# Convolution module of a streaming encoder: shifted copies made inside SBUF, one bank for the layer norm's sums, a new order of steps

## The chip, the cores and the metric

The kernel runs on one core of a Trainium2 chip. The time is the device time of one execution in microseconds (us), launch to end; a run's number is that of one execution, and the median of several runs is compared. TensorE is called PE, VectorE DVE, ScalarE ACT, GpSimd POOL and SyncE SP in the rows. SP computes nothing here: its queue starts every DMA.

## The reference

One step of an encoder with four layers, on 512 new tokens of one stream and 64 of another (576 columns in all), width 1024, float32. Each layer is a token mixer and a feed-forward block. The mixer of layer 1 is the convolution module that the change touches:

```
a, g = split(h @ w_pw1 + b_pw1)           # 1024 -> 2 x 1024
glu  = a * sigmoid(g)
xp   = concat([state, glu])               # 30 earlier rows in front
c    = silu(layernorm(dwconv31(xp)))      # 31 taps for each channel, layer norm over channels
y    = c @ w_pw2 + b_pw2                  # state out: the last 30 rows of xp
```

Layers 0 and 3 attend in a window, layer 2 is a gated MLP; every layer is followed by a feed-forward block with a convolution of width 3.

## The kernel before, in words

Channels lie on the 128 partitions, tokens along the free axis; a matrix of width 1024 is eight tiles c = 0 to 7 of 128 channels. The tokens are worked on in two halves of 256 and 320 columns. Matrix products are made in three passes of a split float32 format (lines 287 to 289): weights arrive by DMA in a stage buffer (two of them), ACT casts the high part (L256), DVE subtracts it for the low part (L259), and PE multiplies high by high, high by low and low by high, for eight slices of the contraction: 24 matmuls a product.

**The convolution module** (`conv_module`, L1272). For each tile c there are four products of pw1 (two halves by two branches). DVE scales each pair by the norm ("turn", L1313), ACT takes the sigmoid (L1316) and DVE gates (L1322) into the gated tile `v_glu`, 636 columns: 30 zeros, the prompt, 30 columns of state, the sample. The 31 taps are split. The first `4 * CPACKS[c]` run on PE in packs of four taps: for channel rows 32q to 32q+31 a copy `cp[q]` (`v_g` in the rows) holds each of the 32 rows four times, shifted by 0, 1, 2 and 3 columns, on 128 partitions, so that one matmul with a weight of 128 x 32 (a stack of four diagonals, made by DVE on L1380 from `ident4` and the columns of taps in `ct`) does four taps of 32 channels; four such matmuls, q = 0 to 3, run side by side in PE's column groups (L1404). The remaining taps run on DVE, one instruction of 606 columns each (L1395), the first of them on ACT (L1393). DVE then joins both parts (L1420).

The copies go by DRAM: one DMA writes the gated tile to `v_gd` (L1373), four DMAs read it back (L1366), each with the source pattern of 4 shifts by 32 rows by w columns.

For the layer norm over channels PE sums the joined tile and its squares with a weight of ones (L1448) into two PSUM banks, one for each half, values in rows 0 to 63 and squares in rows 64 to 127. After four tiles a rough centre is taken off (L1459, L1462, L1465); PE adds it for the later tiles (L1411 to L1413). At the end ACT copies the sums, PE transposes them, DVE works out mean and deviation, and pw2 follows.

**The order of the work** in this module is written out by hand: `CORDER` is a list of steps, a letter and a tile (a third part is a repeat count), and each engine gets its instructions in that order. The letters: R the last part of the norm (R0 steps of its chain on DVE, R1 its spread on PE, R2 a copy on ACT), H and h the load and cast of pw1's weights, l their low part, x one product, t, i, g turn, sigmoid and gate, c the write to DRAM, C the four copies, y the diagonals, b the first DVE tap (on ACT), d a tap on DVE, e a pack on PE, w the centre on PE, j the join, r and v the state's rows, m, n, u the centre, z and q squares and sums, W, O, o load, cast and low part of pw2's weights, K the table of silu. DMAs are started by SP in the order of the list as well; a DMA that has to wait holds those behind it.

PSUM has six banks for products and packs and two for the rest; 20 large buffers hold gated tiles, copies, DVE's results and joined tiles.

Of the kernel before, what the change touches and what calls it, by code (L numbers as in the profile page):

```python
# [8 lines left out]
F32 = mybir.dt.float32  # L9
# [14 lines left out]
NF = 22  # L24
NEG = -1.0e30
APART = 1
CPACKS = (5, 4, 4, 4, 4, 4, 4, 3)

CORDER = (
# [9 lines left out]
)  # L39

AORDER = (
# [92 lines left out]
def encoder_step_kernel(  # L134
# [31 lines left out]
    def mm_tile(name):  # L166
        return mmp.tile([P, 512], F32, tag="mm", name=name)

    def ms_tile(name):
        return msp.tile([P, 512], F32, tag="ms", name=name)  # L170
# [4 lines left out]
    def b_tile(name, shape, dt=F32):  # L175
        return bp.tile(shape, dt, tag="b", name=name)
# [4 lines left out]
    def w_tile(name, shape, dt=F32):  # L181
        return wp.tile(shape, dt, tag="t", name=name)
# [5 lines left out]
    ident = cp.tile([P, P], F32, tag="ident", name="ident")  # L188
    make_identity(nc, ident)
    ident4 = cp.tile([P, 32], F32, tag="ident4", name="ident4")  # L190
    G.tensor_tensor(ident4, ident[:, :32], ident[:, 32:64], ALU.add)
    for q in (64, 96):
        G.tensor_tensor(ident4, ident4, ident[:, q : q + 32], ALU.add)
    ones = cp.tile([P, P], F32, tag="ones", name="ones")
    G.memset(ones, 1.0)
    thirty2 = cp.tile([P, 1], F32, tag="thirty2", name="thirty2")
# [1075 lines left out]
    def conv_module(i, j):  # L1272
# [9 lines left out]
                packs.append((dram(conv_w_dw[j], c * P + q * 32, [[4 * D, np_], [D, 4], [1, 32]]), np_))  # L1282
        ct = columns(f"{n}_ct", [rows(conv_b_pw1, 16), rows(conv_b_dw, 8), rows(conv_ln_g, 8), rows(conv_ln_b, 8), rows(conv_b_pw2, 8), (conv_w_dw[j].rearrange("w (c p) -> (w c) p", p=P), 248), *packs], at)
        wt = ct[:, 48:296].rearrange("p (w c) -> p w c", c=8)
        stt = columns(f"{n}_st", [(state_conv[j, 0].rearrange("w (c p) -> (w c) p", p=P), 240)], 240, tag="mix").rearrange("p (w c) -> p w c", c=8)
        gl, po = {}, []
        halves, place = {}, {}
# [56 lines left out]
        class Tile:  # L1344
# [15 lines left out]
            def copies(self):  # L1360


                w = NB + self.te - 4
                self.cp = [b_tile(f"{self.m}_g{q}", [P, w]) for q in range(4)]
                for q in range(4):
                    nc.sync.dma_start(  # L1366
                        self.cp[q],
                        bass.AP(self.gd.tensor, self.gd.offset + 32 * q * 636, [[1, 4], [636, 32], [1, w]]),
                    )

            def out(self):
                self.gd = dp.tile([P, 636], F32, tag=f"glu{self.c}", name=f"{self.m}_gd")
                nc.sync.dma_start(self.gd, self.g)  # L1373

            def diagonals(self):
                self.dg = []
                for q in range(2):
                    o, np_ = four[self.c] + 2 * q * self.packs, 2 * self.packs
                    t = h_tile(f"{self.m}_dg{q}", F32)[:, : np_ * 32].rearrange("p (n m) -> p n m", m=32)
                    V.tensor_tensor(t, ident4[:, None, :].to_broadcast([P, np_, 32]), ct[:, o : o + np_, None].to_broadcast([P, np_, 32]), ALU.mult)  # L1380
                    self.dg += [t[:, : self.packs], t[:, self.packs :]]

            def tap(self, kind):
# [58 lines left out]
            def squares(self):  # L1442

                if not squared:
                    sums.extend(mm_tile(f"{n}_sums{hf}") for hf in range(2))
                for z, (a, e) in enumerate(((0, 256), (256, NT))):
                    for at, t in enumerate((ds[self.c], self.sq)):
                        T.matmul(  # L1448
                            sums[z][64 * at : 64 * at + 64, : e - a], ones[:, :64], t[:, a:e],
                            start=(not squared), stop=(len(squared) == KD - 1),  # L1450
                        )
                squared.add(self.c)
# [46 lines left out]
        def do(kind, c):  # L1499
            if kind == "K":  # L1500
                S.activation(sp.tile([P, 1], F32, tag="mu", name=f"{n}_silu"), ones[:, :1], AF.Silu)
            elif kind == "R":
                if c == 0:
                    r_steps.pop(0)()
                elif c == 1:
                    steps.append(spread(f"{h.name}_1", h.r[1], 1))
                else:
                    S.copy(half(h.R, 1), steps.pop())
            elif kind in "mnu":
                if kind == "m":  # L1510
                    steps.append(centre())
                next(steps[0])
            elif kind == "H":
                q = asked[c] = asked.get(c, -1) + 1
                load(f"{n}_{c}_w{q}", conv_w_pw1[j], 0, KD, q * D + c * P, P)
            elif kind == "h":
                split(c, ws.setdefault(c, []))
            elif kind == "l":
                lows[c].pop(0)(V)
            elif kind == "W":  # L1520
                load(f"{n}_w2{c}", conv_w_pw2[j], 0, KD, c * P, P)
            elif kind == "O":
                split(("o", c), out_ws.setdefault(c, []))
            elif kind == "o":
                lows["o", c].pop(0)(V)
            elif kind == "x":
                hs = halves.setdefault(c, [])
                if not hs:
                    begin_gated(c)
                if not hs or not hs[-1].products:  # L1530
                    hs.append(Gated(c, len(hs), ws[c]))
                hs[-1].products.pop(0).all()
            elif kind in "tig":
                at = place.get((kind, c), 0)
                place[kind, c] = at + 1
                {"t": Gated.turn, "i": Gated.sigmoid, "g": Gated.gate}[kind](halves[c][at])
            else:
                t = tile_of(c)
                {
                    "b": t.vector, "c": t.out, "C": t.copies, "d": t.vector, "e": t.tensor, "y": t.diagonals, "w": t.tensor_end,  # L1540
                    "j": t.join, "r": t.state, "v": t.rows, "z": t.square, "q": t.squares,
                }[kind]()

# [18 lines left out]

        with tc.manual_schedule(engines={*ENGINES, mybir.EngineType.Activation}):
            rb, db, chains, dr = {}, {}, [], {}
            for hf in range(2):
                w, nb = HALF[hf][1], 2 + hf
                both = b_tile(f"{n}_both{hf}", [P, w])
                S.copy(both, sums[hf][:, :w])
                ps = ms_tile(f"{n}_both{hf}_t")
                for q, at in enumerate((0, P, 192)[:nb]):  # L1570
                    T.transpose(ps[:, q * P : (q + 1) * P], both[:, at : at + P], ident)
                s1, s2 = (ps[:, : nb * P].rearrange("p (b c) -> p b c", c=P)[:, :, at] for at in (0, 64))
                dm, d2, vr, dr[hf] = (sp.tile([P, 3], F32, tag=tag, name=f"{n}_{tag}{hf}")[:, :nb] for tag in ("dm", "d2", "vr", "dr"))
                r, steps_ = rsqrt_steps(f"{n}_s{hf}", vr, nb, 1.0 / D, 1e-5)
                rb[hf] = r
                chains.append([
                    lambda dm=dm, s1=s1: V.tensor_scalar(dm, s1, 1.0 / D, None, ALU.mult),
                    lambda dm=dm, s1=s1, d2=d2: V.tensor_tensor(d2, dm, s1, ALU.mult),
                    lambda vr=vr, s2=s2, d2=d2: V.tensor_tensor(vr, s2, d2, ALU.subtract),
                    *steps_,  # L1580
                    lambda dm=dm, r=r, t=dr[hf]: V.tensor_tensor(t, dm, r, ALU.mult),
                ])
# [321 lines left out]
```

## Time and profile before

| | |
|---|---|
| median of 3 runs | 2830.97 us (2828.22 to 2831.78) |
| profiled execution | 2828.47 us |
| its span, first to last instruction | 2826.7 us |
| PE busy | 2758.0 us, 98% of the span |
| DVE busy | 1857.0 us, 66% |
| ACT busy | 1137.7 us, 40% |
| DMA | 233.31 MB, 83 GB/s in the mean |

In the profile a row names the line, the engine, the operation and the tiles (result first); a bracket tells how long the engine was idle before and what ended that. A matmul in float32 shows as two instructions. [...]

### The profile page before, as it was taken

Reading aid. Unit: us, or ns where it says so; the run is one execution under the profiler, and the core shown is the slowest. Engines: PE = TensorE matmul, PEld = TensorE weight load, DVE = VectorE, ACT = ScalarE, POOL = GpSimd, SP = SyncE. Lnnn points to the kernel's source line nnn. Section 1 sums busy time; section 2 is a strip of 40 time slices with the busy share of each in tenths; the row PEclk is TensorE's granted clock in tenths of the full one; section 3 lists DMA queues with packets and bytes.
Section 4 is the critical chain, followed back from the end, with each engine's and each line's share of the span. In section 5 each row is a group of like instructions: output and inputs, shape, how many; then the busy total and the mean of one; then the engine's idle time right before and its main releaser. Section 6 shows DMA issues by size and latency. Waiting matters only on the chain.

```text
span 2826.7 us, 52768 instructions
## 1 busy us (share of the span) xinstructions
PE 2758.0 (98%) x20841; PEld 2633.4 (93%) x20841; DVE 1857.0 (66%) x4194; ACT 1137.7 (40%) x2392; POOL 384.7 (14%) x937
## 2 busy tenths in 40 slices
PE   8999999999887999999999999999999999999998
PEld 7889999998666899999999999999999878999998
DVE  5668666657776576667657667666666676766674
ACT  4755433334124453233434324432333674533343
POOL 3122111110000021111002011211110121211111
PEclk9999999999888999999999999999999999999999
DMA  5322322322431232222233221322222421322221
GB/s 168 86 52 71 93 87 75 90 66 64 124 119 47 75 90 83 83 84 86 68 91 101 75 77 55 90 83 82 85 81 79 106 50 47 95 86 82 83 83 58
DMA packets 358413, 233.31 MB, mean 83 GB/s; under 512 B 42802, under 2 KB 347670, under 8 KB 358038
## 3 DMA queue, kind: packets, MB, share of 16 engines
q1 hardware_dynamic: 358166, 229.94, 28.0%
q8 instruction: 164, 2.69, 0.4%
q14 instruction: 83, 0.68, 0.1%
HBM read 223.00 MB, written 10.05 MB: 82 GB/s over the span
## 4 chain that ended last, share of the span: by engine, by line
PE 92%; DMA 4%; DVE 2%; SPq 1%; issue 1%; ACT 0%; POOL 0%; POOLq 0%; ACTq 0%; DVEq 0%
PE f_p L287 13%; PE f_p L289 13%; PE f_p L288 13%; PE o_p L287 10%; PE o_p L288 9%; PE o_p L289 9%; DMA v_g<-v_gd 3%; PE v_pc L1404 1%; PE m_u_p L287 1%; PE m_u_p L289 1%; PE m_u_p L288 1%; PE m_vp L287 1%; PE t_sp L1117 1%; PE m_vp L288 1%; PE m_vp L289 1%; PE t_qp L287 1%
## 5 line engine op out<-in xcount | busy, mean ns | idle before, releaser
L287 PE MATMUL f_p<-n_hi,f_w_h 128*128 128x320 f32 (+1 forms) x2688 | 799.1, 297 | 0.0
L289 PE MATMUL f_p<-n_hi,f_w_l 128*128 128x320 f32 (+1 forms) x2688 | 797.3, 297 | 0.0
L288 PE MATMUL f_p<-n_lo,f_w_h 128*128 128x320 f32 (+1 forms) x2688 | 797.3, 297 | 0.0
L287 PEld LDWEIGHTS f_p<-n_hi,f_w_h 128*128 128x128 f32 x2688 | 510.0, 190 | 4.5 <-issue 4.1
L288 PEld LDWEIGHTS f_p<-n_lo,f_w_h 128*128 128x128 f32 x2688 | 510.1, 190 | 0.0
L289 PEld LDWEIGHTS f_p<-n_hi,f_w_l 128*128 128x128 f32 x2688 | 510.0, 190 | 0.0
L287 PE MATMUL o_p<-f_ah,f_d_h 128*128 128x256 f32 (+1 forms) x1408 | 419.5, 298 | 2.8 <-ACT f_d_h L256 2.8
L288 PE MATMUL o_p<-f_al,f_d_h 128*128 128x256 f32 (+1 forms) x1408 | 418.4, 297 | 0.0
L289 PE MATMUL o_p<-f_ah,f_d_l 128*128 128x256 f32 (+1 forms) x1408 | 417.4, 297 | 0.0
L256 ACT CAST f_w_h<-f_w_f 128x512 fp32r<-128x512 f32 x352 | 200.7, 618 | 495.7 <-PE f_p L288 235.8
L537 DVE TENSOR_TENSOR o_y<-o_p,o_y 128x256 f32<-128x256 f32 (+1 forms) x432 | 195.2, 455 | 262.5 <-PE o_p L289 261.2
L800 DVE TENSOR_TENSOR f_ub<-f_p,n_R 128x256 f32<-128x256 f32 x352 | 148.3, 423 | 286.6 <-PE f_p L289 282.0
L287 PEld LDWEIGHTS o_p<-f_ah,f_d_h 128*128 128x128 f32 x1408 | 268.6, 191 | 4.5 <-ACT f_d_h L256 2.9
L288 PEld LDWEIGHTS o_p<-f_al,f_d_h 128*128 128x128 f32 x1408 | 268.7, 191 | 0.2 <-issue 0.2
L289 PEld LDWEIGHTS o_p<-f_ah,f_d_l 128*128 128x128 f32 x1408 | 268.2, 191 | 0.2 <-issue 0.2
L259 DVE TENSOR_TENSOR f_w_l<-f_w_f,f_w_h 128x512 fp32r<-128x512 f32 x352 | 229.1, 688 | 19.8 <-ACT f_w_h L256 17.6
L256 ACT CAST f_d_h<-f_d_f 128x512 fp32r<-128x512 f32 x176 | 101.3, 619 | 231.8 <-PE f_p L288 171.4
L812 DVE SCALAR_TENSOR_TENSOR f_c<-f_ub,f_ct,f_c 128x578 f32<-128x578 f32 x176 | 144.0, 821 | 38.3 <-ACT f_c L811 38.3
L808 POOL COPY f_fo<-f_ub 128x2 f32<-128x2 f32 x176 | 46.1, 262 | 888.2 <-DVE f_ub L800 880.8
L811 ACT ACTIVATE f_c<-f_ub,f_ct 128x578 f32<-128x578 f32 x176 | 150.9, 863 | 1.4 <-POOL f_fo L808 0.7
L821 ACT CAST f_ah<-f_a 128x576 fp32r<-128x576 f32 x88 | 59.3, 674 | 218.6 <-DVE f_a L818 218.6
L813 DVE SCALAR_TENSOR_TENSOR f_c<-f_ub,f_ct,f_c 128x578 f32<-128x578 f32 x176 | 143.5, 817 | 2.8
(374 smaller groups left out, 5632.0 us busy)
## 6 DMA issues: line engine op xcount, KB each, us to landing
f_w_f<-in_ffn_w_up_dram SPq DMA_DIRECT2D x176, 512.0 KB
f_d_f<-in_ffn_w_down_dram SPq DMA_DIRECT2D x80, 512.0 KB
v_w_f<-in_conv_w_pw_dram SPq DMA_DIRECT2D x24, 512.0 KB
t_wq_f<-in_attn_w_qkv_dram SPq DMA_DIRECT2D x32, 256.0 KB
t_wo_f<-in_attn_w_o_dram SPq DMA_DIRECT2D x32, 256.0 KB
m_wv_f<-in_cmlp_w_in_dram SPq DMA_DIRECT2D x16, 512.0 KB
m_u_w_f<-in_cmlp_w_in_dram SPq DMA_DIRECT2D x16, 512.0 KB
m_wo_f<-in_cmlp_w_out_dram SPq DMA_DIRECT2D x16, 512.0 KB
```

The source lines that it names most:

```text
L256: S.copy(hi[:, a:e], st[:, a:e])
L259: eng.tensor_tensor(lo[:, a:e], st[:, a:e], hi[:, a:e].bitcast(F32), ALU.subtract)
L287: T.matmul(ps, lh, rh, start=(i == 0), stop=False)
L288: T.matmul(ps, lh, rl, start=False, stop=False)
L289: T.matmul(ps, ll, rh, start=False, stop=(i == n - 1))
L537: V.tensor_tensor(ys, ps, ys, ALU.add)
L800: V.tensor_tensor(ub[q][:, b : b + 256], ps[q]()[:, :256], h.R[:, hf * 256 : hf * 256 + 256], ALU.mult)
L808: G.tensor_copy(fo[:, 0, :, c], ub[q][:, 512:514])
L811: S.activation(y, ub[q][:, 2:580], AF.Identity, bias=ct[:, 3, c : c + 1], scale=ct[:, 2, c : c + 1])
L812: V.scalar_tensor_tensor(y, ub[q][:, 1:579], ct[:, 1, c : c + 1], y, ALU.mult, ALU.add)
L813: V.scalar_tensor_tensor(y, ub[q][:, 0:578], ct[:, 0, c : c + 1], y, ALU.mult, ALU.add)
L821: S.copy(a_hi[p], am)
```

## The change

The gated tile is no longer written to DRAM: four DMAs copy from SBUF to SBUF, one for each block of 32 channel rows, with a source pattern of 32 rows by 4 shifts by w columns. Row r of the block, shifted by s, now lies on partition 4r + s of the copy (before: 32s + r), so that the four shifts of a row are neighbours. `ident4` and the columns of taps are permuted to match: a permutation matrix `pm` is built from the identity, one matmul reorders the columns into `tp`, once. Tile 6 has three packs on PE instead of four, so four more of its taps run on DVE. The layer norm's sums of both halves go into four groups of 32 rows of one PSUM bank. `CORDER` is rewritten, without the step c.

```diff
-CPACKS = (5, 4, 4, 4, 4, 4, 4, 3)
+CPACKS = (5, 4, 4, 4, 4, 4, 3, 3)
 CORDER = (
-    "y0 H2 R09 y2 R1 y1 R2 H2 y4 t0 h2 t1 i0 l2 i1 g0 l2 h2 r0 c0 g1 b0 x2 l2 b1 l2 c1 d0 v0 d0 r1 d0 C0 x2 v1 d03 x2 d04 "
...
-    "z5 x7 O2 o22 e6 O3 t7 i7 o3 e6 g7 o3 b7 c7 e6 d7 e6 d72 q5 d7 C7 d72 r7 w6 d72 r6 q4 d7 v6 v7 d76 e7 d72 e7 d7 j6 e7 "
-    "z6 w7 q6 j7 z7 q7 K0"
+    "R0 H2 R08 y0 R1 y1 R2 t1 H2 t0 i1 h2 g1 y2 r1 i0 l2 b1 C1 l2 g0 h2 d1 r0 d1 b0 x2 v0 l2 v1 l2 d0 x2 d03 C0 d0 x2 d04 "
+    "x2 d0 t2 d1 i2 g2 d1 e1 H3 t2 e1 d1 i2 g2 e1 d1 b2 H3 d1 e0 d1 h3 d1 e0 d12 e0 d1 h3 e0 d12 e0 l32 e1 C2 j0 l3 x3 j1 "
+    "l3 d2 x3 d24 x3 t3 H4 d2 i3 d22 x3 d2 H4 d22 h4 d2 e2 l42 e2 d2 H5 h4 d2 e2 l42 e2 g3 H5 y5 t3 r2 h5 x4 j2 v2 l5 i3 l5 "
+    "g3 H6 h5 x4 y3 y7 b3 l52 C3 r3 t4 x4 v3 d3 i4 g4 d33 x4 h6 d34 x5 H6 t4 d3 i4 g4 x5 d3 b4 C4 d32 h6 d3 e3 t5 d3 e3 i5 "
+    "g5 y4 e3 l62 e3 l62 r4 H7 j3 x5 v4 d43 H7 d4 m0 d4 h7 d4 l72 d4 W0 x5 n1 d42 u0 x6 h7 l7 z1 l7 z3 t5 W1 q1 d4 q3 z0 i5 "
+    "d4 q0 z2 g5 x6 d4 b5 C5 d4 d5 r5 t6 q2 v5 d5 i6 x6 g6 d54 x6 O0 d54 e4 O1 t6 e4 d5 i6 g6 e5 d52 e5 d5 o0 e5 o0 o1 W2 "
+    "e5 o1 d4 w5 b6 y6 d6 e4 W3 j5 e4 d6 z5 d6 w4 d6 C6 d6 x7 j4 d6 z4 d6 x7 d63 x7 d6 t7 d6 i7 g7 d6 x7 O2 d64 e6 O3 t7 d6 "
+    "i7 e6 g7 o2 b7 e6 o2 d7 q4 C7 d7 w6 d7 r7 d7 r6 d7 q5 v6 j6 v7 d7 z6 d7 q6 d76 e7 d72 e7 d7 e7 d72 w7 o32 j7 z7 q7 K0"
 )
...
-    G.tensor_tensor(ident4, ident[:, :32], ident[:, 32:64], ALU.add)
-    for q in (64, 96):
-        G.tensor_tensor(ident4, ident4, ident[:, q : q + 32], ALU.add)
+    by_four = ident.rearrange("p (m s) -> p m s", s=4)
+    G.tensor_tensor(ident4, by_four[:, :, 0], by_four[:, :, 1], ALU.add)
+    for q in (2, 3):
+        G.tensor_tensor(ident4, ident4, by_four[:, :, q], ALU.add)
...
+        pm = w_tile(f"{n}_pm", [P, P])
+        V.tensor_copy(pm.rearrange("p (r s) -> p r s", s=4), ident.rearrange("p (s r) -> p r s", s=4))
+        pps = ms_tile(f"{n}_tp_ps")
+        T.matmul(pps[:, : at - 296], pm, ct[:, 296:at], start=True, stop=True)
+        tp = sp.tile([P, at - 296], F32, tag="tp", bufs=1, name=f"{n}_tp")
+        S.copy(tp, pps[:, : at - 296])
...
                 for q in range(4):
-                    nc.sync.dma_start(
-                        self.cp[q],
-                        bass.AP(self.gd.tensor, self.gd.offset + 32 * q * 636, [[1, 4], [636, 32], [1, w]]),
-                    )
-
-            def out(self):
-                self.gd = dp.tile([P, 636], F32, tag=f"glu{self.c}", name=f"{self.m}_gd")
-                nc.sync.dma_start(self.gd, self.g)
+                    src = self.g[32 * q : 32 * q + 32, 0:w]
+                    nc.sync.dma_start(self.cp[q], bass.AP(src.tensor, src.offset, [src.ap[0], [1, 4], [1, w]]))
...
-                    V.tensor_tensor(t, ident4[:, None, :].to_broadcast([P, np_, 32]), ct[:, o : o + np_, None].to_broadcast([P, np_, 32]), ALU.mult)
+                    V.tensor_tensor(t, ident4[:, None, :].to_broadcast([P, np_, 32]), tp[:, o : o + np_, None].to_broadcast([P, np_, 32]), ALU.mult)
...
-                    sums.extend(mm_tile(f"{n}_sums{hf}") for hf in range(2))
+                    sums.append(mm_tile(f"{n}_sums"))
                 for z, (a, e) in enumerate(((0, 256), (256, NT))):
                     for at, t in enumerate((ds[self.c], self.sq)):
+                        g = 64 * z + 32 * at
                         T.matmul(
-                            sums[z][64 * at : 64 * at + 64, : e - a], ones[:, :64], t[:, a:e],
+                            sums[0][g : g + 32, : e - a], ones[:, :32], t[:, a:e],
...
+            both = b_tile(f"{n}_both", [P, 320])
             for hf in range(2):
-                w, nb = HALF[hf][1], 2 + hf
-                both = b_tile(f"{n}_both{hf}", [P, w])
-                S.copy(both, sums[hf][:, :w])
-                ps = ms_tile(f"{n}_both{hf}_t")
-                for q, at in enumerate((0, P, 192)[:nb]):
-                    T.transpose(ps[:, q * P : (q + 1) * P], both[:, at : at + P], ident)
-                s1, s2 = (ps[:, : nb * P].rearrange("p (b c) -> p b c", c=P)[:, :, at] for at in (0, 64))
+                S.copy(both[64 * hf : 64 * hf + 64, : HALF[hf][1]], sums[0][64 * hf : 64 * hf + 64, : HALF[hf][1]])
+            ps = ms_tile(f"{n}_both_t")
+            for q in range(2):
+                T.transpose(ps[:, q * P : (q + 1) * P], both[:, q * P : (q + 1) * P], ident)
+            T.transpose(ps[:, 320:384], both[64:128, 192:320], ident[64:128, 64:128])
+            for hf in range(2):
+                nb = 2 + hf
+                s1, s2 = (ps[:, : nb * P].rearrange("p (b c) -> p b c", c=P)[:, :, at + 64 * hf] for at in (0, 32))
```

## Rows read from the trace of the kernel before

**Rows 1.** The page's first part: busy us, share of the span, instructions.

```profile
PE 2758.0 (98%) x20841; PEld 2633.4 (93%) x20841; DVE 1857.0 (66%) x4194; ACT 1137.7 (40%) x2392; POOL 384.7 (14%) x937
```

**Rows 2.** Windows: stretch, length, engines' busy us (x), PEclk, DMA share, GB/s.

```profile
699.55:884.07 184.52, 152.33 (x1208) 117.03 (x1208) 141.19 (x224) 38.88 (x70) 2.46 (x8) 0.87 0.38 117
...
693.00:884.00 191.00, 154.43 (x1220) 118.64 (x1220) 147.39 (x245) 41.94 (x75) 2.46 (x8) 0.87 0.37 113
...
1000.00:1060.00 60.00, 60.00 (x454) 60.00 (x454) 41.46 (x77) 28.68 (x54) 13.43 (x34) 1.00 0.33 97
```

**Rows 3.** Waits of PE's two rows, 690 to 890: us, times, longest.

```profile
PEld v_pc L1404 <- DMA v_g<-v_gd: 34.9, 12, 3.9
...
PE v_pc L1404 <- DMA v_g<-v_gd: 26.9, 11, 3.3
```

**Rows 4.** Waits of VectorE, 693 to 884.

```profile
DVE v_w_l L259 <- ACT v_w_h L256: 12.5, 4, 6.4
DVE v_t L1313 <- PE v_p L289: 7.3, 7, 2.5
DVE v_d L1420 <- PE v_pc L1411: 5.9, 1, 5.9
DVE v_d L1420 <- PE v_pc L1404: 5.8, 4, 3.1
...
DVE v_t L1313 <- PE v_sums L1448: 3.5, 1, 3.5
```

**Rows 5.** A window with copies alone; DMA view of 745 to 752 in 40 slices.

```profile
872.00:875.00 3.00, 1.06 (x2) 0.18 (x2) 2.75 (x6) 0.09 (x1) 0.00 (x0) 0.50 0.24 92
...
DMA  3222222222222222222222259999422222234456
GB/s 97 82 85 99 99 85 113 99 99 85 99 113 99 85 99 113 99 85 99 113 99 85 99 200 419 419 375 419 172 85 99 113 99 85 99 106 150 159 155 176
```

**Rows 6.** Timeline of SyncE's queue (start, us), the last tile.

```profile
857.17 0.35 SPq L1373 DMA_DIRECT2D v_gd<-v_glu  x1
...
860.14 2.79 SPq L1366 DMA_DIRECT2D v_g<-v_gd  x4
```

**Rows 7.** Timeline of PE: packs of tiles 1 and 7, sums of a tile.

```profile
737.59 4.29 PE L1404 MATMUL v_pc<-v_g,v_dg 128*32 128x256 f32 x64
...
859.03 0.43 PE L1448 MATMUL v_sums<-v_d,ones 128*64 128x256 f32 x1
...
859.79 0.43 PE L1448 MATMUL v_sums<-v_sq,ones 128*64 128x320 f32 x1
...
866.05 1.06 PE L1404 MATMUL v_pc<-v_g,v_dg 128*32 128x256 f32 x2 [3.12 <-DMA v_g<-v_gd]
...
875.24 4.80 PE L1404 MATMUL v_pc<-v_g,v_dg 128*32 128x256 f32 x42 [1.97 <-DMA v_g<-v_gd]
```

**Rows 8.** Timeline of VectorE: norm's chain, 18 taps, last join.

```profile
693.07 0.16 DVE L345 TENSOR_SCALAR n_v<-n_c 128x3 f32<-128x3 f32 x1 [5.40 <-PE n_c L373]
...
858.11 15.91 DVE L1395 SCALAR_TENSOR_TENSOR v_cv<-v_glu,v_ct,v_cv 128x606 f32<-128x606 f32 x18 [0.42 <-ACT v_cv L1393]
...
881.31 0.56 DVE L1420 TENSOR_TENSOR v_d<-v_pc,v_cv 128x256 f32<-128x256 f32 x2 [0.17 <-PE v_pc L1413]
```

**Rows 9.** Chain that ended last, 640 to 960 (start, us): tile 0's diagonals.

```profile
672.05 0.40 DVE v_dg L1380
...
673.31 0.40 DVE v_dg L1380
```

**Rows 10.** Timelines of ScalarE and VectorE at the stage's end.

```profile
882.66 1.28 ACT L1501 ACT_TABLE_LOAD   x1
...
884.07 0.68 ACT L1568 COPY v_both<-v_sums 128x256 f32<-128x256 f32 x2
...
884.95 0.16 DVE L1577 TENSOR_SCALAR v_dm<-v_both_t 128x2 f32<-128x2 f32 x1 [3.08 <-PE v_both_t L1571]
```

**Rows 11.** Timeline of PE behind the module's columns.

```profile
633.57 0.58 PE L287 MATMUL o_p<-f_ah,f_d_h 128*128 128x256 f32 x1 [2.77 <-ACT f_d_h L256]
```

More of the change, by code (lines that the diff above doesn't have):

```diff
@@ L1377, in diagonals @@
                 for q in range(2):
-                    o, np_ = four[self.c] + 2 * q * self.packs, 2 * self.packs
+                    o, np_ = four[self.c] - 296 + 2 * q * self.packs, 2 * self.packs
                     t = h_tile(f"{self.m}_dg{q}", F32)[:, : np_ * 32].rearrange("p (n m) -> p n m", m=32)
-                    V.tensor_tensor(t, ident4[:, None, :].to_broadcast([P, np_, 32]), ct[:, o : o + np_, None].to_broadcast([P, np_, 32]), ALU.mult)
+                    V.tensor_tensor(t, ident4[:, None, :].to_broadcast([P, np_, 32]), tp[:, o : o + np_, None].to_broadcast([P, np_, 32]), ALU.mult)
                     self.dg += [t[:, : self.packs], t[:, self.packs :]]
@@ L1539, in do @@
                 {
-                    "b": t.vector, "c": t.out, "C": t.copies, "d": t.vector, "e": t.tensor, "y": t.diagonals, "w": t.tensor_end,
+                    "b": t.vector, "C": t.copies, "d": t.vector, "e": t.tensor, "y": t.diagonals, "w": t.tensor_end,
                     "j": t.join, "r": t.state, "v": t.rows, "z": t.square, "q": t.squares,
```

6 rows, old and new, of the table CORDER are left out of this document.

## The prediction

> **What bounds the kernel now.** I read the busy shares first: PE works 98% of the span [rows 1], so in most of the kernel nothing but PE's own work could matter. The windows by stage then show where the missing 2% lies: in 699.55 to 884.07, the body of the convolution module, PE is busy 152.3 of 184.5 us at a granted clock of 0.87, while a dense stretch of the next layer gives 60.0 of 60.0 at 1.00 [rows 2]. So the change is worth what this stage can lose, and I looked for the wait that ends last there. PE's waits have one large cause: it waits 34.9 + 26.9 = 61.8 us (some of it counted on both of PE's rows) for the shifted copies v_g that come back from DRAM [rows 3]. VectorE is the other heavy engine: 147.4 us busy of 191.0 [rows 2]. Its five largest waits in the stage come to 12.5 + 7.3 + 5.9 + 5.8 + 3.5 = 35.0 us [rows 4], and all five end on PE, or on a cast whose weights came late. Smaller waits are left as they are.
>
> The copies themselves: while only they move, 16 DMA engines are busy 0.24 of the time at 92 GB/s; the write of a gated tile to DRAM and its neighbours reach 419 GB/s with a share of 9 tenths, and the slices around them show 2 tenths at 85 to 113 [rows 5]. So a copy runs on four of sixteen engines. For the last tile: the write is issued at 857.17, the copies at 860.14 [rows 6], and PE gets them at 866.05 (first) to 875.24 (last), one per 3.06 us [rows 7]: 18.1 us from the tile to the last copy.
>
> **The change part by part.** *DRAM hop and copies.* Eight writes and the wait for each go: 860.14 - 857.17 = 3.0 us a tile [rows 6]. The source pattern's outer dimension becomes 32 rows instead of 4 shifts, so I expect all sixteen engines, and the rate of the write, some 400 GB/s [rows 5]: 309 KB in 0.8 us instead of 3.06. The last copy would then land after four issues (2.8 us together [rows 6]), the 2.4 us that the first copy took beyond its issue (0.5) and its 3.06 (866.05 - 860.14 = 5.9), and 0.8: 6 us after the gate, not 18. Bounds: 6 us, and 15.1 (875.24 - 860.14, old rate, no hop). I take 6.
>
> The trace shows no DMA that reads 32 rows of SBUF alone, so the rate of one row of a view is all I have. [...]
>
> *Is the copy then ever waited for?* I walked the new order with the durations below, one running total for each engine. Gate of a tile to its first pack on PE: 17 us for tile 1, about 14 for 0, 2 and 3 (21 for 2), over 30 for 4, 12 for 5, 17 for 6, 7.7 for 7 (gate at 829, and PE is held until 836.9 by tile 6's last sums). All exceed 6, so the copies drop out of the path, and so does what followed them: joins that waited for packs, and weight loads that stood behind copies on four engines and held the casts. That is the 35.0 us of [rows 4].
>
> *VectorE is late next.* One pack of tile 6 moves from PE to VectorE: four taps of 15.91/18 = 0.88 [rows 8], +3.5 us; tile 6's smaller diagonals, -0.1. On PE a pack costs 4.29/4 = 1.07 [rows 7]; saved, but not on the path. The two diagonals of tile 0 stood ahead of the norm's chain, 0.40 us each on the path [rows 9]; behind R0 they lie in the wait for the spread. I count +0.8 for VectorE's list and -0.4 for the stretch ahead (bounds 0 and -0.8: ScalarE also has a turn there). VectorE's list is then 881.9 - 693.1 = 188.8 us from the norm's chain to the last join [rows 8], less 35.0, plus 4.2: 158.0 with the small waits left in.
>
> *PE's list:* 24 products of 24 matmuls at 60.0/454 us each [rows 2], 3.17 a product, 76; 31 packs, 33; the rest (centre, about, state, sums) some 18: 127 us from about 701.5, against VectorE's 158 from 692.7. PE leads VectorE by only 1.4 to 4 us at most turns after tile 2. One new wait I found: tile 0's state transposes now stand behind its gate (about 701.3) and ahead of tile 2's products on PE, 1.8 us later than now. Four products with a restart at half clock end at 716.8; VectorE arrives for tile 2's second turn at 715.7. With 0.1 to 0.2 at the spread: +1.3. Behind PE's wait stand all of tile 2's products; nothing else needs PE then.
>
> *SP's queue.* A copy now waits for its gate where the write did. Behind C1 stand the state rows and C0, behind C5 the weights W2 and W3, behind C7 only state rows. W2 and W3 need the stage that VectorE frees after o0 and o1, near 807; C6 behind them is used at 823. No cost.
>
> *Sums in one bank.* Per tile eight instructions from 859.03 to 860.22 [rows 7]: 1.2 us of PE, 0.55 if all four groups of 32 columns run side by side as the packs do. On PE between 0 and -5 us in all; on the path 0, as PE is ahead. It also frees one PSUM bank. *The tail:* the silu table (882.66) precedes both copies of the sums, and VectorE's chain starts at 884.95, after the first copy and two transposes [rows 10]. Now both copies and three transposes come first: half of the copies' 0.68 more, and one transpose: +0.4 (bounds +0.2, +0.8).
>
> *Setup.* One permuting copy, one matmul, one copy back. The matmul must follow the copy of the columns on ScalarE; PE idles 2.77 us just there for late weights [rows 11], which covers it. If that cover fails, it is a ScalarE round trip of about 1 us. I take +0.3. The strided adds of ident4 run once at the start on POOL: 0.
>
> **Sum.** -35.0 + 3.5 - 0.1 + 0.8 - 0.4 + 1.3 + 0.4 + 0.3 = -29.2 us. The profiled execution took 2828.47 us (span 2826.7), 2.5 below the median 2830.97: so 2799.3, or 2801.8 from the median. I forecast **2800**, its own range 2794 to 2806. A floor: VectorE idles 191.0 - 147.4 = 43.6 us [rows 2], 2.1 of them behind the last join [rows 8]; without any of these 41.5 and without the new 1.3 it would be 2799.3 - 6.5 - 1.3 = 2791.5.
>
> **The rivals.** *A, PE too slow for the lead:* PE's lead is 1.4 to 4 us, and each restart costs that: 42 matmuls in 4.80 us after a wait against 64 in 4.29 [rows 7]. If the stage kept its clock of 0.87 [rows 2], 127 becomes 146 from 701.5, ending at 847, close to VectorE's 692.7 + 158.0 = 850.7; two nearly equal engines waiting in turn give back 8 to 14 us: **2811**. For: the short idle spells remain. Against: the long ones (3 us each) go.
>
> *B, the new copies still run on few engines:* then only the hop goes. Tile 7's copies land at 829 + 15 = 844, its packs run at half clock, tiles 5 and 7 come some 3 us late together, and the casts again wait for weights behind copies (VectorE's 12.5 [rows 4]): saved 29.2 - 12.5 - 3 = 14, **2814**. For: the destination's shape is as before. Against: the change of the outer dimension. [...]
>
> *C, slower than before:* copies from SBUF to SBUF are slower than from DRAM. They all go through one queue; eight sets from 699.5, then 8.8 us as from 875.24 to 884.07, reach the old end at T = (884.07 - 8.8 - 699.5)/8 = 22 us a set. Below about 18 us most of the saving stays; at 25 the stage ends at 908, **2853**. For: four overlapping reads of each row, seen nowhere here. Against: it needs 58 GB/s, under the 92 of today, and the write of the same tile out of SBUF is among the fastest transfers of the stage [rows 5].
>
> **Chances.** Forecast 0.66, A 0.14, B 0.11, C 0.09 (a third of it within 0.2% of before, where T is near 22). What this kernel's measurement can tell from no change is about 0.2%, 5.7 us; so faster 0.91, same 0.03, slower 0.06. The range takes the forecast and most of A and B: 2792 to 2817.
>
> **What would show it.** Right: no wait of PE on v_g; copies at a DMA share well over 0.25; weights no longer late for the casts; VectorE busy over 95% from the norm's chain to the last join, which ends near 852; stage clock nearer 1. Wrong: waits of turns for products of several us each (A), a share of 0.25 beside the copies (B), waits for copies on every tile (C).

## The result, and the profile after

The changed kernel takes **2793.77 us** (median of 4 runs, 2793.27 to 2795.66) against 2830.9 us before (4 runs, 2828.22 to 2831.78): ratio **0.987, 95% interval 0.9857 to 0.9885**, 37.1 us less. The profiled execution took 2793.36 us. Its first rows, the span and the busy shares that answer to [rows 1]:

```profile
span 2791.6 us, 52728 instructions
...
PE 2740.8 (98%) x20825; PEld 2622.4 (94%) x20825; DVE 1858.2 (67%) x4199; ACT 1137.2 (41%) x2393; POOL 386.9 (14%) x937
```

The stage is best cut where VectorE's work in it begins and ends: from the norm's chain to the end of the last join. For the kernel before, the window view gives (columns as in [rows 2]):

```profile
693.07:881.87 188.80, 152.34 (x1210) 117.82 (x1211) 147.39 (x245) 39.93 (x72) 2.46 (x8) 0.86 0.37 114
```

and for the changed kernel, where the chain starts at 692.30 and the last join ends at 843.40 + 0.88 = 844.28:

```profile
692.30:844.28 151.98, 135.39 (x1197) 107.81 (x1197) 148.58 (x251) 39.66 (x72) 1.71 (x8) 0.95 0.49 121
```

VectorE (third pair) is busy 148.58 of 151.98 us: it idles 3.4 us, where it idled 41.4. PE works 17 us less, at a granted clock of 0.95 instead of 0.86 (PEclk, third from the right: the share of TensorE's full clock that was granted). VectorE's waits in this stretch that answer to [rows 4] are gone: the waits view of 692.30 to 844.28 has one row left, and that one ends where the stretch begins.

```profile
DVE n_v L345 <- PE n_c L373: 5.4, 1, 5.4
```

Of PE's waits for copies [rows 3], 61.8 us, this is what is left (692 to 845); PE now waits for VectorE:

```profile
PEld v_sums L1450 <- DVE v_d L1421: 9.7, 2, 5.2
...
PEld v_pc L1405 <- DMA v_g<-v_glu: 0.6, 1, 0.6
```

The stage's end, to be held against [rows 8, 10]: last join, both copies of the sums behind the table load, PE's transposes, VectorE's chain, the spread on PE, first product of pw2.

```profile
843.40 0.88 DVE L1421 TENSOR_TENSOR v_d<-v_pc,v_cv 128x256 f32<-128x256 f32 x3
...
845.02 1.28 ACT L1503 ACT_TABLE_LOAD   x1
...
846.42 0.78 ACT L1569 COPY v_both<-v_sums 64x256 f32<-64x256 f32 x2
...
848.28 0.16 DVE L1581 TENSOR_SCALAR v_dm<-v_both_t 128x2 f32<-128x2 f32 x1 [4.00 <-PE v_both_t L1573]
...
850.66 1.22 PE L385 MATMUL v_rd<-ident,v_s_o 128*128 128x128 f32 x4 [2.42 <-DVE v_s_o L353]
...
854.78 0.58 PE L287 MATMUL o_p<-v_chi,v_w_h 128*128 128x256 f32 x1 [2.05 <-ACT v_chi L1605]
```

The same two PE rows before:

```profile
887.41 0.68 PE L385 MATMUL v_rd<-ident,v_s_o 128*128 128x128 f32 x4 [2.07 <-DVE v_s_o L353]
...
890.59 0.58 PE L287 MATMUL o_p<-v_chi,v_w_h 128*128 128x256 f32 x1 [2.05 <-ACT v_chi L1601]
```

With these the 35.1 us between the two profiled executions add up: chain's start 692.30 - 693.07 = -0.8; stage 151.98 - 188.80 = -36.8; last join to first product of pw2 10.50 - 8.72 = +1.8; from there to the span's end 1936.8 - 1936.1 = +0.7.

### The profile page after: what moved, and what is told of

The parts are those of the page before. It is cut to its first block, busy times and chain, and to the rows that moved or that the text cites. A ratio compares the mean times of both kernels' runs of the same rounds, so it can differ in the third digit from the quotient of the medians.

```text
span 2791.6 us, 52728 instructions
## 1 busy us (share of the span) xinstructions
PE 2740.8 (98%) x20825; PEld 2622.4 (94%) x20825; DVE 1858.2 (67%) x4199; ACT 1137.2 (41%) x2393; POOL 386.9 (14%) x937
## 4 chain that ended last, share of the span: by engine, by line
PE 90%; DVE 7%; DMA 1%; issue 1%; ACT 1%; SPq 0%; POOL 0%; POOLq 0%; DVEq 0%; ACTq 0%
PE f_p L287 13%; PE f_p L289 13%; PE f_p L288 13%; PE o_p L287 10%; PE o_p L288 10%; PE o_p L289 10%; DVE v_cv L1396 3%; PE m_u_p L287 1%; PE m_u_p L289 1%; PE m_u_p L288 1%; PE m_vp L287 1%; PE m_vp L288 1%; PE m_vp L289 1%; PE t_o L1178 1%; PE t_sp L1117 1%; PE t_qp L287 1%
## 5 line engine op out<-in xcount | busy, mean ns | idle before, releaser
L287 PE MATMUL f_p<-n_hi,f_w_h 128*128 128x320 f32 (+1 forms) x2688 | 799.8, 298 | 0.0
L287 PEld LDWEIGHTS f_p<-n_hi,f_w_h 128*128 128x128 f32 x2688 | 510.4, 190 | 4.5 <-issue 4.1
L287 PE MATMUL o_p<-f_ah,f_d_h 128*128 128x256 f32 (+1 forms) x1408 | 419.6, 298 | 2.2 <-ACT f_d_h L256 2.2
L287 PEld LDWEIGHTS o_p<-f_ah,f_d_h 128*128 128x128 f32 x1408 | 268.5, 191 | 4.0 <-ACT f_d_h L256 2.5
```

The costliest lines, as they stand in the source:

```text
L287: T.matmul(ps, lh, rh, start=(i == 0), stop=False)
```

## The experiments

Times are medians, with the range of the runs; every kernel was timed beside the kernel before, whose medians were 2831.7 (first four kernels), 2831.1 (next four) and 2830.3 (last four). "Stage" is the length of the stretch above in each kernel's own trace; it is that of one execution, and two executions of one program differed by 2.0 us in it (b3 and d4 below).

**Which part did it: pattern, way through DRAM, or order?** Three kernels take the parts one at a time. *b1* is the kernel before with the copies' source pattern turned round and nothing else (the rows of the diagonals follow):

```diff
-  bass.AP(self.gd.tensor, self.gd.offset + 32 * q * 636, [[1, 4], [636, 32], [1, w]])
+  bass.AP(self.gd.tensor, self.gd.offset + 32 * q * 636, [[636, 32], [1, 4], [1, w]])
```

> The kernel before, with its order, its pack counts, its two banks and its copies through DRAM, and one thing changed: the copies' pattern has the 32 rows as its slowest dimension instead of the 4 shifts (with the row order of the diagonals that this needs). Theory (how many engines carry a copy is the whole cause; the way through DRAM costs nothing by itself): as the SBUF copies in the same order, 2794 to 2799 us, and VectorE's waits between its chain and the last join fall from 41 us to under 12. Rival (the hop through DRAM comes on top in the old order, since each set can be issued only 2.3 to 5 us after the gate): 2803 to 2815. Rival (order and pattern need one another): above 2815.

Measured: 2796.15 us (2795.58 to 2797.66), ratio 0.9877 [0.9863, 0.9890]; stage 155.12, in which VectorE idles 155.12 - 145.99 = 9.1 us, under the 12 expected. The theory holds: this one line is worth 35.0 of the 37.1 us. *a1* is the kernel before with the copies made inside SBUF, in the old order, old packs, two banks:

```diff
-  bass.AP(self.gd.tensor, self.gd.offset + 32 * q * 636, [[1, 4], [636, 32], [1, w]]),
+  src = self.g[32 * q : 32 * q + 32, 0:w]
+  nc.sync.dma_start(self.cp[q], bass.AP(src.tensor, src.offset, [src.ap[0], [1, 4], [1, w]]))
```

> The copies alone: the order of steps of before (only the step c is dropped), its packs and its two banks of sums, but the gated tile copied inside SBUF. Theory (the stage is bound by VectorE's list, and needs both short copies and an order that keeps PE ahead): PE's waits for copies and the casts that waited for late weights go (5.9 + 5.8 + 12.5 us of VectorE's idle time), the waits of turns for products (7.3 + 3.5) stay or grow: 15 to 26 us faster than before, some 2805 to 2816 us. Rival 'the order did it': 0 to 8 us faster. Rival 'the copies did it all': 33 us faster or more, some 2795.

Measured: 2796.27 us (2795.51 to 2797.03), ratio 0.9876 [0.9862, 0.9889]; stage 155.26. Less than my theory's 2805 to 2816: the old order did not need to be rewritten to profit. And it equals b1 within 0.1 us, so leaving DRAM is worth nothing here. *a3* asks the same in the new order: the changed kernel with its copies read back from DRAM, 32 rows as the slowest dimension, and the write behind each tile's last gate.

```diff
-  src = self.g[32 * q : 32 * q + 32, 0:w]
-  nc.sync.dma_start(self.cp[q], bass.AP(src.tensor, src.offset, [src.ap[0], [1, 4], [1, w]]))
+  bass.AP(self.gd.tensor, self.gd.offset + 32 * q * 636, [[636, 32], [1, 4], [1, w]])
```

> The new order with the gated tile by DRAM, but the source pattern of the copies with 32 rows outermost (the changed kernel's layout of the copies). Tells the engines from the hop. If the number of engines is what matters: DMA share near 1 beside the copies, a set lands 3 us (the hop) later than in the changed kernel or earlier where DRAM gives its rows faster than SBUF (today 155 to 160 GB/s): 0 to 4 us slower than the changed kernel, 2793 to 2798. If leaving DRAM is what matters: 10 us slower or more, over 2804.

Measured: 2794.98 us (2793.28 to 2795.85), ratio 0.9872 [0.9857, 0.9887]; stage 151.81. Not to be told from the changed kernel. *a2* is a3 with the old pattern, `[[1, 4], [636, 32], [1, w]]`: the new order and one bank, on the old copies.

> The order alone: the new order, packs and one bank of sums, but the gated tile goes by DRAM as before (the write put right behind a tile's last gate, the copies where they stood, on four engines). Theory: a set needs 18 us from gate to last copy; the new order leaves 14 for tiles 0 and 3, 12 for 5 and 7.7 for 7, so PE waits 4 + 4 + 6 + 10 us for copies and casts wait for late weights again: 12 to 25 us slower than the changed kernel, 2806 to 2819. Rival 'the order did it': within 5 us of the changed kernel, under 2799. Rival 'the copies did it all': within 8 us of before.

Measured: 2841.91 us (2840.1 to 2843.78), ratio 1.0037 [1.0024, 1.0049]: slower than before by some 10 us, where my theory had a gain of 12 to 25. Its VectorE waits, from the chain to the last join, say why:

```profile
DVE v_d L1420 <- PE v_pc L1404: 22.8, 4, 15.9
DVE v_d L1420 <- PE v_pc L1411: 12.4, 2, 6.3
DVE v_w_l L259 <- ACT v_w_h L256: 8.6, 1, 8.6
```

The new order puts gates, packs and joins closer together; with copies that take 18 us, joins stand and wait for packs (22.8 + 12.4 = 35.2 us), more than the old order lost there to the same copies [rows 4]. PE starts on tile 7's four copies at 875.00, 878.09, 881.09 and 884.12, one per 3.0 us, as in [rows 7]. So the order is not good or bad by itself: it is written for fast copies.

**How fast are the new copies?** In the trace of the changed kernel tile 7's set (four of 307 KB) is issued from 824.73. Its first pack starts at 831.68, but that time says nothing about the copies: until 830.49 PE stood at tile 6's sums, waiting for VectorE's join. One weight load of tile 7 did wait for a copy:

```profile
833.50 0.27 PEld L1405 LDWEIGHTS v_pc<-v_g,v_dg 128*32 128x32 f32 x8 [0.58 <-DMA v_g<-v_glu]
```

So the set took up to 8.8 us (833.50 - 824.73), not the 6 I had. The DMA view of 826 to 834 in slices of 0.2 us:

```profile
DMA  8979697699999995299888878889957475393357
GB/s 123 135 74 111 74 111 123 209 307 283 233 147 111 111 74 61 49 270 282 233 258 295 307 307 270 233 246 233 219 143 170 182 263 130 102 144 118 100 164 223
```

All engines are busy (share mostly 7 to 9 tenths), and yet the rate is only 49 to 307. The first 33 slices hold the set's 1.23 MB: 186 GB/s over 6.6 us. It isn't a steady rate: the windows 826 to 828, 828 to 830 and 830 to 832 show 155, 157 and 251 GB/s. *c1* reads other rows for each copy, spread over all partitions:

```diff
-  src = self.g[32 * q : 32 * q + 32, 0:w]
+  src = self.g[q::4, 0:w]
```

> The changed kernel, but each copy reads every fourth of the 128 partitions instead of 32 neighbouring ones; the taps that TensorE computes then belong to other channels. Size, engines and target are the same. Theory (the 155 GB/s at the start of a set comes from reading 32 neighbouring partitions): the first 4 us of tile 7's set run at 250 GB/s or more. Rival (a copy from SBUF to SBUF is that slow wherever its rows lie): 140 to 180 GB/s again. The time of the kernel stays at 2792 to 2796 either way, since the copies are off the path.

Measured in one run: 2795.31 us, and in the same window:

```profile
DMA  0000000002999999999999999882039945899986
GB/s 0 0 0 0 0 0 0 0 0 111 405 368 381 393 369 393 393 418 381 393 442 405 393 405 393 267 235 52 3 113 184 177 131 159 261 310 351 346 261 200
```

17 slices from 827.8 hold the set: 361 GB/s over 3.4 us, twice the rate, at the same size, target and queue. SP's queue also takes 2.5 us for the four issues (from 826.75) where the changed kernel's takes 5.0. So it is the 32 neighbouring rows that made the copies slow, as the theory said. The time of this one run did not move, as expected: no wait of PE for a copy is left, and the first pack of tile 7 starts at 833.70, again right behind tile 6's sums.

**Is VectorE the bound now?** *a4* gives tile 6's fourth pack back to PE (four taps fewer on VectorE):

```diff
-CPACKS = (5, 4, 4, 4, 4, 4, 3, 3)
+CPACKS = (5, 4, 4, 4, 4, 4, 4, 3)
```

> The changed kernel with tile 6's fourth pack back on PE: one step e6 more, four taps d6 fewer. Theory (VectorE's list is the bound, it waits 0.6 us in the whole stage): 3.5 us of taps less and nothing else, 3.0 to 3.6 us faster than the changed kernel, 2790 to 2791, the last join 3.5 us earlier. Rival 'PE and VectorE are level' (the pack was moved because PE was the later one): within 1 us of the changed kernel, or slower by the pack's 1.1 us.

Measured: 2790.79 us (2789.64 to 2791.17), ratio 0.9856 [0.9842, 0.9869], 3.0 under the changed kernel; stage 149.46, 2.5 shorter. As the theory said. *b3* does it for tile 7 too:

```diff
-CPACKS = (5, 4, 4, 4, 4, 4, 3, 3)
+CPACKS = (5, 4, 4, 4, 4, 4, 4, 4)
```

> The changed kernel with a fourth pack on TensorE, and four taps fewer on VectorE, for tile 6 and for tile 7. Theory (VectorE is late in the whole stage, four taps are 3.5 us): 2786 to 2788, twice the step of 3.0 us that tile 6 alone gave. Rival (tile 7's packs come last and TensorE is at half clock there, so a pack more ends after VectorE): 2789 to 2793.

Measured: 2781.76 us (2779.67 to 2782.11), ratio 0.9826 [0.9812, 0.9839]: 12.0 under the changed kernel, far outside both. Between the two profiled executions it is 13.7, and the stage accounts for 151.98 - 146.25 = 5.7 of that. The chain also starts 2.1 us earlier (690.24), and everything behind the first product of pw2 is 5.9 us shorter. The group of feed-forward matmuls shows it; first the changed kernel, then b3:

```profile
L287 PE MATMUL f_p<-n_hi,f_w_h 128*128 128x256 f32 x1280 | 362.4, 283 | 0.0
```

```profile
L287 PE MATMUL f_p<-n_hi,f_w_h 128*128 128x256 f32 x1280 | 359.5, 281 | 0.0
```

*d4* is b3 once more, to see whether that comes back:

> The kernel with a fourth pack for tiles 6 and 7 once more. In its first run it was 12.0 us under the changed kernel, of which the stage's own trace gives 5.7; the rest stood in the other stages, where each of the 12288 long matmuls of the feed forward layers took 1 to 2 ns less. Theory (only the stage's gain belongs to the edit): 2785 to 2788 this time. Rival (the other stages' gain comes with this program): 2780 to 2783 again.

Measured: 2779.67 us (2778.59 to 2780.56), ratio 0.9823 [0.9809, 0.9836], and 281 ns again. My theory fell: the gain outside the stage comes with this program. In the stage the two executions differ, though: 148.25 us here, 146.25 in b3. In both PE waits for tile 7's copies before its packs (1.44 and 1.50 us); here the 58 matmuls behind that wait take 6.44 us, in b3 4.27, and the last join waits 1.85 us for them. So the stage's gain is 3.7 to 5.7 us, and the copies from 32 neighbouring rows are waited for again. The gain behind the module appears in all three programs with four packs for tile 7 (b3, which is also d4, d2 and d3) and in none of the others (283 ns). Why a program that differs only in this module runs the feed-forward matmuls 2 ns faster was not found.

*d1* moves VectorE's last two low weight parts behind the last join, where it idles anyway:

```diff
-d72 w7 o32 j7 z7 q7 K0
+d72 w7 j7 z7 q7 o32 K0
```

> The changed kernel with two steps moved: VectorE's last two low weight parts (o3, 0.64 us each) stand behind the last join and its square instead of ahead of them. No work is added or left out. Theory (VectorE is the last to arrive at the last join, and idle for 4 us right behind it): 1.3 us less, 2792.2 to 2792.8. Rival (TensorE's packs of tile 7 arrive at the same time, so the join waits for them): no change, 2793.5 to 2794.

Measured: 2793.91 us (2792.68 to 2794.28): no change, against my theory, and yet not the rival's reason. In the trace the last join begins 11.48 us after the end of tile 6's join, where the changed kernel took 12.51; that is the gain. But this execution had lost 1.03 us long before:

```profile
716.89 0.49 DVE L1320 TENSOR_TENSOR v_t<-v_p,n_R 128x320 f32<-128x320 f32 x1 [1.03 <-PE v_p L289]
```

The same wait stands in the traces of a2, b2 and c1 (1.0 to 1.1 us) and not in those of the changed kernel, a3 and a4. Whether this wait comes and goes between executions of one program, single profiles can't say (b3 and d4, one program, differ there by 0.2 us only), so d1 is inconclusive on its size.

**One bank or two?** *b2* puts the sums back in two banks, as before, in the changed kernel:

```diff
-  sums.append(mm_tile(f"{n}_sums"))
+  sums.extend(mm_tile(f"{n}_sums{hf}") for hf in range(2))
```

> The changed kernel with the layer norm's sums in two banks as before. Theory (the sums are off the path; only the tail counts, where the chain from last join to VectorE took 4.00 us with one bank and 3.08 with two): 2792 to 2794, that is 0 to 1.5 us under the changed kernel. Rival (the 256 extra columns a tile make TensorE late at the joins): 2796 to 2800.

Measured: 2794.11 us (2792.95 to 2796.21), ratio 0.987 [0.9856, 0.9883]: the same as one bank. PE is busy 137.19 us in the stage instead of 135.39, off the path; VectorE's wait behind the last join is 3.61 us instead of 4.00. From the end of the last join to pw2 it takes 857.07 - 847.83 = 9.24 us, 1.26 less than with one bank. The first four matmuls of the norm's spread take 0.68 us here, as in the kernel before, whose granted clock is 1.00 beside them (887.4 to 888.6); in the changed kernel they take 1.22 us, at 0.50 (850.66 to 852.73).

```profile
853.90 0.68 PE L385 MATMUL v_rd<-ident,v_s_o 128*128 128x128 f32 x4 [1.75 <-DVE v_s_o L353]
```

So one bank costs about 1.3 us on the path. The median does not show it; in this execution the stage is 1.1 us longer than the changed kernel's, with the wait of 1.1 us at tile 2's turn that d1 has too.

**A version that is faster than both.** *d2* joins b3 and d1:

> The fourth packs of tiles 6 and 7 and the low weight parts behind the last join together. In the trace with the packs alone, TensorE's last pack of tile 7 ended at 835.5 us and the last join began at 835.61, so both engines arrive together. Theory (TensorE is as late as VectorE there): within 0.6 us of the packs alone, not 1.3 us under. Rival (VectorE alone still sets the end): 1.3 us under the packs alone.

Measured: 2778.89 us (2776.31 to 2782.15), ratio **0.9821 [0.9807, 0.9834]**, 0.8 under d4 with wide ranges: not to be told from it. In its trace VectorE waits for PE at the last join, so both arrive together, as the theory said:

```profile
835.61 0.43 DVE L1421 TENSOR_TENSOR v_d<-v_pc,v_cv 128x256 f32<-128x256 f32 x1 [0.63 <-PE v_pc L1412]
```

*d3* takes four more taps of tile 6 to PE and moves tile 4's last two packs behind tile 7's products:

```diff
-CPACKS = (5, 4, 4, 4, 4, 4, 4, 4)
+CPACKS = (5, 4, 4, 4, 4, 4, 5, 4)
```

> A version meant to be faster: as the last one, with a fifth pack for tile 6, and the last two packs of tile 4 (with its join and square) behind the last products of tile 7, so that tile 7's gate comes some 3 us earlier and TensorE's idle 6 us ahead of tile 7's packs is used. Theory (both engines arrive together, and both get 3 us less ahead of the join): 2 to 4 us under the kernel with fourth packs for tiles 6 and 7. Rival (the late join of tile 4 holds PSUM banks that tile 6's packs wait for): 0 to 4 us over it.

Measured: 2781.31 us (2780.38 to 2781.79), ratio 0.9828 [0.9815, 0.9841], 1.6 over d4: not the gain of 2 to 4 that I expected, and the rival's time. The taps that went had stood ahead of tile 7's second turn, and VectorE now arrives there before PE's products.

```profile
819.93 0.49 DVE L1320 TENSOR_TENSOR v_t<-v_p,n_R 128x320 f32<-128x320 f32 x1 [3.56 <-PE v_p L289]
```

Those products are late too: PE's matmuls of L287 wait 1.4 us for a join of VectorE (those of 256 columns) and 2.0 us for a turn (those of 320 columns), and the latter take 323 ns in the mean instead of 316. d4's trace has neither wait. That fits PSUM banks held by a late join, as the rival had it, though at tile 7's products and not at tile 6's packs; no run separates the two reasons.

So of the versions run, the fourth packs for tiles 6 and 7 (with or without d1's move) are the best: 12 to 15 us under the changed kernel, 49 to 51 under the kernel before. In them PE waits 1.4 to 1.5 us for tile 7's copies; *c1*'s spread rows, which move twice as fast, were not tried there.

## Why the prediction held, and which terms were off

*The number.* 2793.77 us lies in the range of 2792 to 2817, near its lower end; the narrower range of 2794 to 2806 around the forecast of 2800 it misses by 0.2 us.

*The mechanism.* It was right. A DMA share of 0.24 beside the copies [rows 5] I took for four of sixteen engines, and that 32 rows as the outer dimension would give all sixteen was an expectation that no row showed; in b1, where only that is turned, the share is 0.72 to 0.93 beside tile 7's copies (the microseconds 833 to 839). VectorE is the next bound (a4). The 35.0 us of VectorE's five waits went whole. Rival A did not come: PE waits for VectorE (9.7 us at two sums), and the stage's clock rose to 0.95. B did not come in the changed kernel: the DMA share beside tile 7's copies is 0.87 to 0.96 (windows of 2 us from 826 to 832). C had a true core: the changed kernel's copies are slower than those from DRAM (186 GB/s; a3's from DRAM moved 341 to 382 in the microseconds 829 to 833), by their 32 neighbouring rows and not by the way from SBUF to SBUF (c1: 361). But 8.8 us a set is far from the 22 at which it decides. (The rate at 22 us is 56 GB/s, not the 58 that C gives.)

*The rate of the copies.* 400 GB/s and 6 us were wrong: 186 GB/s and up to 8.8 us. I had taken over the rate of the write, which reads all 128 rows; no run shows it for copies from 32 neighbouring ones. The slower copies cost 0.6 us on PE's weight loads at tile 7, whose first pack came 7.0 us after the issue; it is the tile for which I had found the smallest slack, 7.7 us. In the faster versions b3, d2 and d4 the same copies cost PE 1.4 to 1.5 us there.

*The sum.* Forecast -29.2, measured -35.1 between the profiled executions. By place:

| | forecast | measured |
|---|---|---|
| ahead of the stage, with the setup | -0.4 + 0.3 = -0.1 | -0.8 |
| VectorE's waits in the stage | -35.0 + 1.3 = -33.7 | 3.4 - 41.4 = -38.0 |
| VectorE's work in the stage | +4.2 | 148.58 - 147.39 = +1.2 |
| last join to pw2 | +0.4 | +1.8 |
| behind it | 0 | +0.7 |

The step that failed is "smaller waits are left as they are". Nothing but 3.4 us of idle time is left: the small waits (1.8 us for ScalarE's first taps, 0.9 at gates, 0.2 at a join) went with the large ones, 3.0 us, and the new 1.3 us at tile 2's turn is absent from this execution. It was well foreseen, though: it stands in four other traces at 1.0 to 1.1 us, at 716.89 in d1, where I had put it at 715.7 to 716.8.

VectorE's work was mis-sized by 3.0 us. By groups taps and diagonals did grow as forecast (95.1 + 4.9 to 98.3 + 5.7 us, +4.0). But low parts, turns and joins fell by 0.4, 0.5 and 0.4 us, and the overlap of neighbours in the record, which is the sum of the groups less the busy time, grew from 5.6 to 7.1 us: an instruction that follows at once begins before the one ahead has ended (the 13 taps from 830.81 in the changed kernel 0.08 us before the end of the join ahead, 830.01 + 0.88), one behind a wait does not. So the removed waits gave a little more than their length here.

*The tail* was too small. VectorE's wait behind the last join grew by 4.00 - 3.08 = +0.9 instead of +0.4, just past my upper bound of 0.8. Another 0.9 us I had not seen: the spread's eight matmuls take 2.07 us from the first to the last (before: 1.13), with PE at half clock there: the granted clock, third from the right in the window below, is 0.50. It is not PE's idle time ahead of the last join that does it: in b2 PE is idle longer there (5.14 us against 4.33) and the spread takes 0.68 us as before, in b3 PE idles 0.51 us and the spread takes 1.22. It goes with the one bank, which leaves PE less work between join and spread (three transposes instead of five; PE busy 3.33 us in the changed kernel, 4.67 in b2): the changed kernel, b3, c1, d1, d2, d3 and d4, with one bank, all have 1.22 us, the kernel before, b1 and b2, with two, all 0.68. So the one bank costs about 1.3 us in the tail (b2), where the sum had +0.4 for it.

```profile
848.00:856.00 8.00, 3.21 (x11) 2.43 (x12) 5.20 (x25) 2.01 (x5) 0.00 (x0) 0.50 0.00 1
```

The floor of 2791.5 that I named was nearly reached.

*The setup and the start.* The permuting matmul lies inside PE's idle time behind the columns: it waits 1.22 us for its operand there and costs nothing, where I had +0.3. The -0.8 ahead is not shown to come from tile 0's diagonals: the chain starts at 693.21 and 693.22 in a1 and b1, which have them ahead, and at 691.40, 692.95, 693.20, 693.36 and 694.78 in a4, a3, d1, c1 and b2, which do not.

*The order.* I gave it no term of its own; the comparison was with waits that the copies caused. The runs split 37.1 us so: pattern -35.0 (b1), way through DRAM about 0 (a1 against b1), new order with one bank at equal packs 2790.79 - 2796.27 = -5.5 (a4 against a1), the pack moved to VectorE +3.0 (a4). These come to 37.4; the 0.3 too much lies within what the median of the kernel before itself moved between the groups of runs (2830.3 to 2831.7). The pack that the change takes from PE is a loss.

## What to carry to other kernels

Look at the DMA share beside a transfer that somebody waits for: a steady quarter of sixteen engines (0.24) marked the slow copies here, and turning the pattern's dimensions round was worth 1.2% of the whole kernel, in one line, with no change of path or order. When a wait that starves several engines goes, name the engine that is late next and expect even its small waits to vanish; then balance the work between the two engines again, since the split that was tuned around the old wait is no longer the best. An order written for fast transfers can be worse than the old one if the transfers stay slow, so change the transfer first.

## What the runs showed of the hardware

- Engines as busy did not move as much: the same four copies ran at 186 GB/s in the mean from 32 neighbouring SBUF rows (DMA share 0.90 over 826 to 832.6) and at 361 GB/s from 32 rows spread over all partitions (c1; 9 tenths in its slices).
- A DMA's issue on SP's queue took longer for the former, 0.84 us (median of 32) in the changed kernel, than for the latter, 0.57 (median of 32) in c1. A slow transfer alone does not do it: the copies of the kernel before, at 92 GB/s [rows 5], took 0.54.
- With the norm's sums in one bank TensorE's granted clock was 0.50 at the spread behind the last join (changed kernel), with two banks 1.00 (kernel before); its eight matmuls took 2.07 us and 1.13 us.
- The feed-forward matmuls of 256 columns took 281 ns in the programs with four packs for tile 7 and 283 in all others, some 6 us behind the stage; the cause is open.
